# Squares, root and raw weights of a gated MLP prepared during the projection ahead of it, with its output tiles reloaded in four parts

## The chip, the cores and the metric

The kernel runs on one core of one Trainium2 chip. A core has a matrix engine (TensorE, PE in the profile), a vector engine (VectorE, DVE), an activation engine (ScalarE, ACT), a general engine (GpSimd, POOL) and an engine that issues most of the transfers (SyncE, SP). Each works through its own queue of instructions in order; semaphores tie the queues together. The metric is the device time of one execution in microseconds, as the median of several runs.

## The reference, cut to what matters

The model has two layers on x of 1024 rows (S) by 1024 columns (D): a mixer with its output projection, then a gated MLP with a causal convolution of width 3 (ConvGLU, called the FFN here), then a gated embedding add ("ple"). All is fp32.

```python
def rmsnorm(x, g):
    y = x * lax.rsqrt(jnp.mean(x * x, axis=-1, keepdims=True) + NORM_EPS)
    return y * g

def conv_glu(hn, w_in, conv_w, conv_b, w_out):           # FFN = 2816
    u, gate_in = jnp.split(hn @ w_in, 2, axis=-1)
    c = (conv_w[0] * shift_right(gate_in, 2) + conv_w[1] * shift_right(gate_in, 1)
         + conv_w[2] * gate_in + conv_b)
    return (jax.nn.gelu(c, approximate=False) * u) @ w_out

for each layer:
    h = h + mixer(rmsnorm(h, attn_norm))                 # ends in the output projection: o @ w_out
    h = h + conv_glu(rmsnorm(h, ffn_norm), ...)
    e = rmsnorm(p[layer] @ ple_w_proj, ple_norm)
    h = h + jax.nn.sigmoid(rmsnorm(h, ple_gate_norm) @ ple_w_gate) * e
```

## The kernel before

**Layout and split products.** Activations lie transposed: h is one tile of 128 partitions x 8 (the 1024 columns of D, KD = 8) x 1024 rows of the sequence, worked on in two halves of 512 (`lo` and `hi`, BW = 512). An fp32 operand is split into a rounded part and a rest (`split`, L169: a cast on ACT, L171, and a subtraction, L172, on POOL, or on the engine that the caller names). Each product of two operands is three matmuls (`mm3`, L190, recorded at L197): high by high, high by low, low by high.

**Output projection** (`out_proj`, L325). Eight tiles f of 128 output columns, two column blocks b of 512; each result is added into h by DVE at L332. The last three of its sixteen results are of the high half.

**Into the FFN.** `conv_glu` (L417) stores h to DRAM (L425), since the FFN works in the memory in which h lies, and calls `ffn_in` (L506). The product of h and w_in goes by a seven-product scheme on 2x2 blocks, so its operands are seven sums of quarters of the normalised h. `ffn_operands` (L438) makes them: for each half a root (`root`, L452: squares on ACT at L454 and L457, adds on DVE at L458, a matmul with ones at L460, a square root on ACT at L462, a reciprocal of 128x512 on DVE at L464), the normalised quarters (`normed`, L469, eight instructions a half), and then sums (L488, L490, L494, L499) and splits on DVE. The low half gives operands 0 and 1 (tiles `mh`, `ml`), the high half the rest (tiles `x`). The squares take tiles under the tag `x6`, in the pool of the seven operands, which is opened when the projection's operand tiles are freed. The weights get the same treatment in `seven_weights` (L356): raw loads (L363), the sums `s3` and three more on POOL (L375 to L380), and seven splits, two on POOL and five (`w6` and later) on DVE. The raw pool is opened in `ffn_in` too, after the projection.

**Out of the FFN.** `ffn_in` leaves its result u in DRAM (`md`, L548). Then h is loaded again into one tile (L432), after all its memory has come free, and `ffn_out` (L579) goes over u in groups of two tiles: loads `mraw` (L587), splits on POOL, and for each block b and, within it, each tile f a product and an add into h (L598). `ple` (L601) loads p into tiles of the weights' pool (`wraw`, L610) and splits them on POOL.

**Other parts that the change uses.** `sumsq_step` (L125) does one step of a sum of squares. `root` of the class (L146) makes the root otherwise: four narrow matmuls sum over partitions into a 128x4 tile (L149), square root (L151) and reciprocal (L152) work on that, and DVE multiplies it into a diagonal (L154). `spread` (L159) multiplies ones by that diagonal on PE, which puts the root into all 128 partitions of a PSUM tile (L161). `open_tail` (L306) opens the pools, among them `row` with six tiles and eight PSUM banks.

**Order.** The program writes down dependences; a scheduler sets each engine's order at build time, and memory that an earlier pool held can be used once the earlier users are done. `run` (L1665) calls all of this for both layers.

## Time and profile before

| | us |
|---|---|
| time, median of 3 runs | 3083.52 |
| lowest and highest run | 3079.57, 3084.25 |
| the profiled execution's own time | 3088.84 |
| its span | 3086.9 |
| PE busy | 2922.4 (95% of the span) |
| DVE, ACT, POOL busy | 2079.4, 1257.5, 1024.3 |
| mean granted clock of PE | 0.963 of full speed |

The profile is one execution, and its span begins and ends a little inside that execution's own time. The busy shares are over the whole span; the chain of waits and the timeline tell which engine a stretch waits for. The rows of the page and of the trace that matter stand two sections below, in numbered groups.

### The profile page before, as it was taken

What the parts mean: (1) busy time and instruction counts of PE and PEld (TensorE: products, weight loads), DVE (VectorE), ACT (ScalarE), POOL (GpSimd) and SP (SyncE); (2) the same over time, 40 slices, a digit from 0 to 9 for tenths busy, and PEclk for the clock granted to TensorE, in tenths of its full rate; (3) what the DMA queues carried; (4) which work ended last, traced back from release to release, by engine and by line L of the source; (5) the groups of instructions that cost most, each with busy time, mean ns of one, the idle gap of its engine ahead of it and who ended that gap; (6) DMA issues with size and microseconds to landing.
All of it is one profiled execution on the core that took longest, in us unless ns stands there. A gap on an engine that the chain in (4) does not pass through costs nothing. (4 is left out here: it accounts for less than half of the span.)

```text
span 3086.9 us, 40717 instructions
## 1 busy us (share of the span) xinstructions
PE 2922.4 (95%) x14510; PEld 2238.5 (73%) x14510; DVE 2079.4 (67%) x3202; ACT 1257.5 (41%) x2269; POOL 1024.3 (33%) x792
## 2 busy tenths in 40 slices
PE   8999999999599999999998899999789999999997
PEld 6777777678378888788886656556558888878876
DVE  6765657873787666544698677775397777655577
ACT  6433436672343333312544434343244333412274
POOL 4322421212244444544323500011134444544333
PEclk9998989999799999999999899999889999999998
DMA  4344565634122222532121300012212222243211
GB/s 139 115 140 119 156 200 141 157 83 160 48 86 82 82 82 72 181 92 79 62 89 55 110 15 23 19 38 96 72 55 82 82 82 82 97 155 99 62 60 55
DMA packets 221018, 286.07 MB, mean 93 GB/s; under 512 B 62256, under 2 KB 106800, under 8 KB 220816
## 3 DMA queue, kind: packets, MB, share of 16 engines
q1 hardware_dynamic: 215632, 272.99, 29.0%
q10 hardware_dynamic: 5184, 10.49, 0.9%
q8 instruction: 114, 1.87, 0.3%
q14 instruction: 88, 0.72, 0.1%
HBM read 200.50 MB, written 81.79 MB: 91 GB/s over the span
## 5 line engine op out<-in xcount | busy, mean ns | idle before, releaser
L197 PE MATMUL mm<-x,whi 128*128 128x512 f32 x1760 | 561.8, 398 | 17.9 <-DVE x L172 10.5
L172 POOL TENSOR_TENSOR wlo<-wraw,whi 128x512 fp32r<-128x512 f32 (+2 forms) x238 | 319.8, 1350 | 621.2 <-ACT whi L171 506.7
L197 PE MATMUL mm<-mh,whi 128*128 128x512 f32 x1056 | 419.1, 397 | 7.8 <-DVE h L598 7.6
L197 PE MATMUL mm<-mh,wlo 128*128 128x512 f32 x1056 | 418.8, 397 | 2.3 <-POOL wlo L172 2.3
L197 PE MATMUL mm<-ml,whi 128*128 128x512 f32 x1056 | 417.4, 395 | 0.0
L197 PE MATMUL mm<-xh,whi 128*128 128x512 f32 (+1 forms) x1016 | 406.7, 400 | 6.9 <-ACT xh L177 6.7
L197 PEld LDWEIGHTS mm<-x,whi 128*128 128x128 f32 x1760 | 333.1, 189 | 106.4 <-DVE x L172 20.3
L598 DVE TENSOR_TENSOR h<-h,mm 128x512 f32<-128x512 f32 x352 | 241.1, 688 | 237.7 <-PE mm L197 208.0
L197 PE MATMUL mm<-xh,wlo 128*128 128x512 f32 (+1 forms) x1016 | 399.5, 393 | 0.0
L197 PE MATMUL mm<-xl,whi 128*128 128x512 f32 (+1 forms) x1016 | 393.2, 394 | 0.5 <-DVE xl L178 0.5
L197 PE MATMUL mm<-x,wlo 128*128 128x512 f32 x880 | 347.1, 394 | 0.0
L171 ACT CAST whi<-raw 128x512 fp32r<-128x512 f32 x264 | 163.1, 619 | 356.8 <-PE mm L197 317.3
L171 ACT CAST whi<-wraw 128x512 fp32r<-128x512 f32 (+2 forms) x242 | 143.3, 596 | 343.1 <-PE mm L197 305.0
L197 PEld LDWEIGHTS mm<-mh,whi 128*128 128x128 f32 x1056 | 200.7, 190 | 55.9 <-DVE h L598 8.5
L197 PEld LDWEIGHTS mm<-ml,whi 128*128 128x128 f32 x1056 | 200.6, 190 | 47.7 <-issue 1.0
L197 PEld LDWEIGHTS mm<-mh,wlo 128*128 128x128 f32 x1056 | 200.3, 190 | 47.5 <-POOL wlo L172 3.2
L197 PEld LDWEIGHTS mm<-xh,whi 128*128 128x128 f32 x1016 | 195.4, 192 | 53.4 <-ACT xh L177 7.4
L197 PEld LDWEIGHTS mm<-xl,whi 128*128 128x128 f32 x1016 | 194.9, 192 | 46.0 <-issue 4.9
L197 PEld LDWEIGHTS mm<-xh,wlo 128*128 128x128 f32 x1016 | 195.0, 192 | 41.8 <-issue 2.1
L172 POOL TENSOR_TENSOR wlo<-raw,whi 128x512 fp32r<-128x512 f32 x88 | 130.7, 1486 | 270.9 <-ACT whi L171 270.7
L197 PEld LDWEIGHTS mm<-x,wlo 128*128 128x128 f32 x880 | 166.4, 189 | 36.3
L172 DVE TENSOR_TENSOR wlo<-raw,whi 128x512 fp32r<-128x512 f32 x176 | 153.3, 874 | 17.1 <-ACT whi L171 17.1
(414 smaller groups left out, 5234.8 us busy)
## 6 DMA issues: line engine op xcount, KB each, us to landing
raw<-in_ffn_w_in SPq DMA_DIRECT2D x176, 256.0 KB
wraw<-in_ffn_w_out SPq DMA_DIRECT2D x88, 256.0 KB
md<-u SPq DMA_DIRECT2D x88, 256.0 KB
mraw<-md SPq DMA_DIRECT2D x88, 256.0 KB
wraw<-in_hyb_w_in SPq DMA_DIRECT2D x52, 256.0 KB
hs<-h SPq DMA_DIRECT2D x32, 256.0 KB
h<-hs SPq DMA_DIRECT2D x32, 256.0 KB
wraw<-in_ple_w_gate SPq DMA_DIRECT2D x32, 256.0 KB
```

The lines of the kernel that those rows point to most:

```text
L171: nc.scalar.copy(out=hi, in_=src)
L172: (eng or nc.gpsimd).tensor_tensor(out=lo, in0=src, in1=hi, op=OP.subtract)
L197: nc.tensor.matmul(ps, lhsT=w, rhs=x, start=first and i == 0, stop=last and i == len(seq) - 1)
L598: nc.vector.tensor_tensor(out=h[:, f, bs], in0=h[:, f, bs], in1=ps, op=OP.add)
```

## The change

There are five edits. (1) `ffn_operands` makes its sums of squares by `sumsq_step`, with one square tile in the `row` pool, and its roots by `root` and `spread`, so that the normalising instructions read the root from PSUM. (2) The pool of raw weights is opened ahead of the projection's operand and closed after `ffn_in`. (3) The late splits of the weights (five of seven, `late`) go to POOL for the first pair of tiles, and stay on DVE for the others. (4) The h that is reloaded lies in four tiles of two column groups each (`Rows` finds the right one); `ffn_out` goes over f outside and b inside, and the splits of its group 0 (c == 0) go to DVE. (5) `ple` loads p into tiles under the tags `sq` and `sd`. `run` opens the raw pool for layer 1 as the last lines of the diff show it for layer 0.

```diff
+class Rows:
...
+    def __getitem__(self, at):
+        p, k, cols = at
+        if isinstance(k, slice):
+            n = k.start // 2
+            return self.tiles[n][p, slice(k.start - 2 * n, k.stop - 2 * n), cols]
+        return self.tiles[k // 2][p, k % 2, cols]
...
-    def sumsq_step(self, pool, acc, src, first):
+    def sumsq_step(self, pool, acc, src, first, bufs=2):
...
-            sq = pool.tile([P, BW], F32, name="sq", bufs=2)[:, :src.shape[1]]
+            sq = pool.tile([P, BW], F32, name="sq", bufs=bufs)[:, :src.shape[1]]
...
-    def seven_weights(self, wp, rp, srcs):
+    def seven_weights(self, wp, rp, late, srcs):
...
-        def split(x, eng=nc.vector):
+        def split(x, eng=late):
...
+    def open_raw(self, ctx):
+        self.rp = ctx.enter_context(self.tc.tile_pool(reuse_waits="tile", name="raw", bufs=RAWS))
+
-    def conv_glu(self, h, layer, c_h):
+    def conv_glu(self, h, layer, c_h, c_raw):
...
-        h = self.pool_tile(c_h, f"h2_{layer}", "right")
+        c_raw.close()
+        pool = c_h.enter_context(tc.tile_pool(reuse_waits="tile", name=f"h2_{layer}", bufs=1, side="right"))
+        h = Rows([pool.tile([P, 2, S], F32, name=f"h2_{k}") for k in range(0, KD, 2)])
...
             acc = row.tile([P, BW], F32, name="row")
             for k in range(KD):
-                if k == 0:
-                    nc.scalar.activation(out=acc, in_=h[:, k, bs], func=AF.Square)
-                else:
-                    sq = xp.tile([P, BW], F32, name="sq", tag="x6", bufs=KD)
-                    nc.scalar.activation(out=sq, in_=h[:, k, bs], func=AF.Square)
-                    tt(out=acc, in0=acc, in1=sq, op=OP.add)
-            ps = self.pm.tile([P, BW], F32, name="mm")
-            nc.tensor.matmul(ps, lhsT=self.ones, rhs=acc, start=True, stop=True)
-            sd = row.tile([P, BW], F32, name="row")
-            nc.scalar.activation(out=sd, in_=ps, func=AF.Sqrt, scale=1.0 / D, bias=self.eps[:, 0:1])
-            r = row.tile([P, BW], F32, name="row")
-            nc.vector.reciprocal(out=r, in_=sd)
-            return r
+                self.sumsq_step(row, acc, h[:, k, bs], k == 0, 1)
+            return self.spread(self.pm, self.root(row, self.pm, acc, D, tag="row", bufs=6))
...
-        rp = ctx.enter_context(tc.tile_pool(reuse_waits="tile", name="raw", bufs=RAWS))
...
-        def weights(tiles):
-            return self.seven_weights(self.wp, rp, [[w_in[layer, f][:, H * k:H * k + H] for k in range(2)] for f in tiles])
+        def weights(tiles, late=nc.vector):
+            return self.seven_weights(self.wp, self.rp, late, [[w_in[layer, f][:, H * k:H * k + H] for k in range(2)] for f in tiles])
...
-            gates = self.seven(ep, xs, weights([NFT + f for f in tiles]), outs(gate))
+            late = nc.vector if i else nc.gpsimd
+            gates = self.seven(ep, xs, weights([NFT + f for f in tiles], late), outs(gate))
             if i == 0:
 
-                ups = self.seven(ep, xs, weights(tiles), outs(up))
+                ups = self.seven(ep, xs, weights(tiles, late), outs(up))
...
-                    self.split(mh[b], ml[b], raw)
+                    self.split(mh[b], ml[b], raw, eng=None if c else nc.vector)
...
-            for b in range(NBLK):
-                bs = slice(b * BW, (b + 1) * BW)
-                for f in range(KD):
+            for f in range(KD):
+                for b in range(NBLK):
+                    bs = slice(b * BW, (b + 1) * BW)
...
-                praw = wp.tile([P, BW], F32, name="praw", tag="wraw", bufs=self.wbufs[0])
+                praw = sp.tile([P, BW], F32, name="praw", tag=("sq", "sd")[k])
...
-                with ExitStack() as c_op:
-                    self.open_operand(c_op, scratch=False)
-                    self.out_proj("hyb_w_out", o, load(t["x"]), h)
-                h = self.conv_glu(h, 0, c_h)
+                with ExitStack() as c_raw:
+                    self.open_raw(c_raw)
+                    with ExitStack() as c_op:
+                        self.open_operand(c_op, scratch=False)
+                        self.out_proj("hyb_w_out", o, load(t["x"]), h)
+                    h = self.conv_glu(h, 0, c_h, c_raw)
```

What this does to the engines' queues shows in three places. The names: `mh` and `ml` are block tiles (the high and low part of operands 0 and 1, or a gate product), `xh` and `xl` the projection's operand, `whi` and `wlo` split weights, `row` a sum of squares, `sq` a square, `raw` and `s` raw weights and their sums. A row with xN stands for N alike in a row. Lines of the kernel after the change are higher: L211 is L197, L186 is L172, L346 is L332, L147 is L458, L477 is L469.

On PE, from the last product of layer 0's output projection into the FFN's first product, before:

```order
L197 MATMUL mm<-xl,whi 128x512
L197 MATMUL mm<-xh,wlo 128x512
L460 MATMUL mm<-row,ones 128x512 x2
L197 MATMUL mm<-mh,whi 128x512
L197 MATMUL mm<-ml,whi 128x512
L197 MATMUL mm<-mh,wlo 128x512
```

and after:

```order
L211 MATMUL mm<-xl,whi 128x512
L211 MATMUL mm<-xh,wlo 128x512
L163 MATMUL mm<-ones,row 128x1 x4
L175 MATMUL mm<-diag,ones 128x512
L211 MATMUL mm<-mh,whi 128x512
L211 MATMUL mm<-ml,whi 128x512
L211 MATMUL mm<-mh,wlo 128x512
...
L211 MATMUL mm<-mh,wlo 128x512
L163 MATMUL mm<-ones,row 128x1 x4
L175 MATMUL mm<-diag,ones 128x512
L211 MATMUL mm<-x_7760,whi 128x512
```

Both roots (one matmul with ones each) stood together ahead of the FFN's first product; now the first root stands there, and the second stands 24 matmuls (operands 0 and 1) later, ahead of the first matmul of an operand `x`.

On DVE, from the last adds of that projection to the first operand of the high half, before:

```order
L332 TENSOR_TENSOR h<-h,mm 128x512 x16
L458 TENSOR_TENSOR row<-row,sq 128x512 x7
L464 RECIPROCAL row<-row 128x512
L458 TENSOR_TENSOR row<-row,sq 128x512
L469 SCALAR_TENSOR_TENSOR h<-h,cols,row 128x512 x3
...
L469 SCALAR_TENSOR_TENSOR h<-h,cols,row 128x512 x2
L458 TENSOR_TENSOR row<-row,sq 128x512
L172 TENSOR_TENSOR ml<-h,mh 128x512 x2
L458 TENSOR_TENSOR row<-row,sq 128x512
L172 TENSOR_TENSOR wlo<-raw,whi 128x512
L458 TENSOR_TENSOR row<-row,sq 128x512
...
L464 RECIPROCAL row<-row 128x512
```

and after:

```order
L346 TENSOR_TENSOR h<-h,mm 128x512 x3
L166 RECIPROCAL sdt<-sdt 128x4
L168 TENSOR_TENSOR diag<-ident,sdt 128x512
L147 TENSOR_TENSOR row<-row,sq 128x512
L477 SCALAR_TENSOR_TENSOR h<-h,cols,mm 128x512 x3
L186 TENSOR_TENSOR ml<-h,mh 128x512 x3
...
L186 TENSOR_TENSOR ml<-h,mh 128x512 x2
L147 TENSOR_TENSOR row<-row,sq 128x512 x5
L166 RECIPROCAL sdt<-sdt 128x4
L168 TENSOR_TENSOR diag<-ident,sdt 128x512
L477 SCALAR_TENSOR_TENSOR h<-h,cols,mm 128x512 x2
```

The adds of the squares of the low half have moved up among the adds into h; of the high half's adds five stand together behind the splits of the low half, and the weight splits that stood between them are gone from this place.

On POOL, at the start of layer 0's projection (L1477 and L1582, after it L1486 and L1591, are the end of the mixer: copies, and products with the gate), before:

```order
L1477 COPY stacks<-stacks 64x256 x10
L172 TENSOR_TENSOR wlo<-wraw,whi 128x512 x2
L1582 TENSOR_TENSOR ml<-ml,gate 128x512
L172 TENSOR_TENSOR wlo<-wraw,whi 128x512
L1582 TENSOR_TENSOR ml<-ml,gate 128x512
L172 TENSOR_TENSOR wlo<-wraw,whi 128x512
L1582 TENSOR_TENSOR ml<-ml,gate 128x512
L172 TENSOR_TENSOR wlo<-wraw,whi 128x512 x2
L1582 TENSOR_TENSOR ml<-ml,gate 128x512
L172 TENSOR_TENSOR wlo<-wraw,whi 128x512 x10
L375 TENSOR_TENSOR s_7954<-raw 128x512
```

and after:

```order
L1486 COPY stacks<-stacks 64x256 x10
L389 TENSOR_TENSOR s_7966<-raw 128x512
L390 TENSOR_TENSOR raw<-raw 128x512
L186 TENSOR_TENSOR wlo<-wraw,whi 128x512 x2
L1591 TENSOR_TENSOR ml<-ml,gate 128x512
L186 TENSOR_TENSOR wlo<-wraw,whi 128x512
L1591 TENSOR_TENSOR ml<-ml,gate 128x512
L186 TENSOR_TENSOR wlo<-wraw,whi 128x512
L1591 TENSOR_TENSOR ml<-ml,gate 128x512 x2
L186 TENSOR_TENSOR wlo<-wraw,whi 128x512 x12
L186 TENSOR_TENSOR wlo<-raw,whi 128x512
```

Two sums of raw weights have moved from behind the projection's weight splits to the front, and the fifth split of a projection weight has moved from ahead of the last gate product to behind it.

## Rows read from the trace of the kernel before

**Rows 1.** The page, part 1: busy us, share of the span, instructions

```profile
PE 2922.4 (95%) x14510; PEld 2238.5 (73%) x14510; DVE 2079.4 (67%) x3202; ACT 1257.5 (41%) x2269; POOL 1024.3 (33%) x792
```

**Rows 2.** Waits of PE by releaser: line waited for: us in total, times, longest

```profile
PE mm L460 <- DVE row L458: 56.8, 4, 20.8
...
PE mm L197 <- DVE h L598: 7.6, 2, 4.0
...
PE mm L197 <- POOL wlo L172: 2.3, 2, 1.3
```

**Rows 3.** Timeline, PE, layer 0: start, us, instruction, count [idle before <-releaser]

```profile
790.04 2.07 PE L460 MATMUL mm<-row,ones 128*128 128x512 f32 x2 [7.04 <-DVE row L458]
...
812.95 2.08 PE L460 MATMUL mm<-row,ones 128*128 128x512 f32 x2 [20.84 <-DVE row L458]
...
854.33 0.50 PE L197 MATMUL mm<-x,whi 128*128 128x512 f32 x1 [0.24 <-DVE x L172]
```

**Rows 4.** Timeline, DVE, the same stretch

```profile
783.65 6.34 DVE L458 TENSOR_TENSOR row<-row,sq 128x512 f32<-128x512 f32 x7
...
796.69 2.06 DVE L469 SCALAR_TENSOR_TENSOR h<-h,cols,row 128x512 f32<-128x512 f32 x3
...
807.40 0.69 DVE L458 TENSOR_TENSOR row<-row,sq 128x512 f32<-128x512 f32 x1
...
820.43 1.41 DVE L469 SCALAR_TENSOR_TENSOR h<-h,cols,row 128x512 f32<-128x512 f32 x2
...
824.22 1.76 DVE L469 SCALAR_TENSOR_TENSOR h<-h,cols,row 128x512 f32<-128x512 f32 x1
...
840.37 4.27 DVE L172 TENSOR_TENSOR x<-h,x 128x512 fp32r<-128x512 f32 x4 [1.64 <-ACT x L171]
```

**Rows 5.** Timeline, ACT, the same stretch

```profile
784.37 0.63 ACT L457 ACTIVATE sq<-h 128x512 f32<-128x512 f32 x1 [15.77 <-DVE row L458]
```

**Rows 6.** Timeline, POOL, the same stretch

```profile
810.02 4.00 POOL L375 TENSOR_TENSOR s<-raw 128x512 f32<-128x512 f32 x1 [13.90 <-DVE wlo L172]
...
822.62 2.81 POOL L172 TENSOR_TENSOR wlo<-raw,whi 128x512 fp32r<-128x512 f32 x1 [7.26 <-ACT whi L171]
```

**Rows 7.** Timeline, PE, narrow matmuls of a root elsewhere in the kernel

```profile
1710.89 1.05 PE L149 MATMUL mm<-ones,row 128*128 128x1 f32 x8 [0.56 <-DVE row L133]
```

**Rows 8.** Lines L151, L154, L161: xcount: ns min/median/max, first and last start, forms

```profile
L151 ACT ACTIVATE sdt<-mm,eps x5: 262/263/264, 1712.0 to 3077.4; 128x4 f32<-128x4 f32 x3, 128x2 f32<-128x2 f32 x2
...
L154 DVE TENSOR_TENSOR diag<-ident,sdt x5: 424/692/1057, 1712.5 to 3077.9; 128x512 f32<-128x512 f32 x3, 128x256 f32<-128x256 f32 x2
...
L161 PE MATMUL mm<-diag,ones x10: 544/592/766, 1721.2 to 3079.1; 128*128 128x512 f32 x6, 128*128 128x256 f32 x4
```

**Rows 9.** Timelines, SP, POOL, DVE, PE, start of layer 0's projection

```profile
676.14 15.16 SPq L183 DMA_DIRECT2D wraw<-in_hyb_w_out  x4
...
700.64 2.99 POOL L172 TENSOR_TENSOR wlo<-wraw,whi 128x512 fp32r<-128x512 f32 x2
703.60 1.74 POOL L1582 TENSOR_TENSOR ml<-ml,gate 128x512 f32<-128x512 f32 x1
...
699.45 1.95 DVE L1579 SCALAR_TENSOR_TENSOR ml<-tr,cols,bv 64x256 f32<-64x256 f32 x4
...
703.06 0.39 PE L197 MATMUL mm<-xh,whi 128*128 128x512 f32 x1
703.28 0.39 PE L197 MATMUL mm<-xh,wlo 128*128 128x512 f32 x1
```

**Rows 10.** Timeline of SP, then the chain that ended last, layer 1

```profile
2700.04 0.94 SPq L587 DMA_DIRECT2D mraw<-md  x2
2702.75 9.52 SPq L432 DMA_DIRECT2D h<-hs  x16
...
2694.15 1.74 POOL wlo L172
...
2697.82 4.85 DMA md<-u
```

14 lines of the change are left out of this document (9 added, 5 removed).

## The prediction

> **What bounds the kernel now.** I read the busy shares first: TensorE (PE) is busy 95% of a span of 3086.9 us, so whatever the change gains has to come out of PE's idle time [rows 1]. Next the waits of PE by releaser. The largest by far is the root matmul of the FFN waiting for the sum of squares, 56.8 us in four waits; the change touches two more, 7.6 us at the start of ffn_out (for h) and 2.3 us at the start of ple (for a split on POOL) [rows 2]. Then the timeline, to see what these waits are made of. In layer 0 PE ends the output projection at 783.0 (790.04 less 7.04), waits 7.04 us for the first root and, after it, 20.84 us for the second [rows 3]. On DVE that stretch is seven adds (from 783.65, 6.34 us), root, splits of the low half until 807.40, five more adds, a reciprocal of 128x512, and at 820.43 the first operand of the high half [rows 4]. ACT shows the cause of the late adds: its squares could not start before 784.37, after 15.77 us of idle, though the low half of h is complete some 16 us before the projection ends (three results of the high half, 24 matmuls of 0.22 us each, come behind it [rows 9]): each has a tile in memory that the projection's last matmul still reads [rows 5]. From 820.43 DVE makes the high half's operands back to back, and PE runs dry behind it in small steps until 854.33 [rows 3, 4]. So the bound between 783.0 and 854.33 is DVE's chain, not PE, and time is won only by what brings 854.33 forward. Layer 1 repeats it: the other two of the four waits are 56.8 - 7.04 - 20.84 = 28.9 us.
>
> **Squares and root of the low half.** After the change the seven adds stand among the adds of the projection, ahead of its last three, so at 783.0 the sum is there. The root is now four narrow matmuls, 1.05 us [rows 7], a square root of 128x4, 0.26, a reciprocal of that size, for which I take 0.2 (between nothing and the square root's 0.26), the diagonal, 0.69, and the spreading matmul, two passes of 0.59 that overlap, about 1.0 [rows 8]: 3.2 us, 3.4 with the handoffs. The low half starts at 783.0 + 3.4 = 786.4 instead of 796.69, 10.3 us sooner. In layer 1 the square root needs an activation table to be loaded, and it does in the kernel before too; there I take the same gain.
>
> **The low half's splits** take 807.40 - 796.69 = 10.7 us [rows 4]; I add 1.0 us for one POOL instruction that falls into them (see below): end at 798.1.
>
> **Squares of the high half.** One tile makes square and add alternate: 0.63 + 0.69 and about 0.1 of handoff, 1.4 us a step [rows 4, 5], where before the squares lay ready and DVE put a late split between two adds. Five adds are left after the low half. The first is ready; the second's square stands on ACT behind a weight cast that waits for PE to finish the second product. I estimate that it ends 3.5 us after the first begins, and three steps follow: 798.1 + 3.5 + 4.2 = 805.8. The root's 3.4 us give 809.2 for the first high operand, against 820.43: 11.2 us sooner. The 24 matmuls of products 0 and 1, which stood behind the second root, now run between the roots, in time in which PE idles anyway.
>
> **The high half** takes 854.33 - 820.43 = 33.9 us now [rows 3, 4]. Two late splits of 0.6 us leave DVE for POOL: -1.2. A POOL instruction beside dense DVE work is not free: while POOL's ran for 2.81 us in place of 1.3 to 1.5 [rows 6, 9], the DVE instruction at 824.22 took 1.76 us, where three of its kind in 2.06 are 0.69 each [rows 4]. That is 1.0 us a piece, and I count two more of them than now: +2.0. PE has five more matmuls behind the last operand, since its order is another, at 0.22 us each [rows 9]: +1.1. Net 11.2 + 1.2 - 2.0 - 1.1 = 9.3 us a layer, **18.6 us in two**. Bounds: with no collision and without the stall of 1.64 us in today's phase [rows 4], 17 us a layer; with 4.0 us for every POOL instruction, as at 810.02 [rows 6], and a high half that waits for them, 3 us.
>
> The trace thus shows DVE and POOL delaying each other by about 1 us an instruction [rows 4, 6]. The Trainium skill ("SBUF — State Buffer", the reading of its diagram) says why this speaks against moving splits to POOL: the SBUF port pair that the two share is an exclusive lock, and the later of a GpSimd instruction and a DVE instruction with two SBUF inputs waits for the whole of the other. By that rule alone a split moved from DVE's 0.6 us costs DVE up to a POOL instruction's 1.3 to 1.5, and the sum would be some 2 us smaller for each layer; the rows agree with the rule in kind.
>
> **Early raw weights.** They remove loads from behind the last store of h; POOL's two sums of them move from behind the projection into its idle time. That costs something at layer 0's projection start, where the order on POOL changes: the split of the fifth weight tile now stands behind the last gate product (1.74 us at 703.60), not ahead of it [rows 9]. PE wants that split at 703.28; today it ends at about 702.1 (half of 2.99 after 700.64). With the product from 701.4, when DVE has made its input (699.45 plus 1.95), to 703.1, it ends at 704.6 [rows 9]: **+1.4 us**, bounds 0 and 4. The three raw loads now ahead of the first projection weights I count at nothing: those weights go out at 676.14, 27 us before that split is wanted [rows 9], and a load is worth about 1 us.
>
> **h in four tiles, and the order of ffn_out.** Today the reload goes out at 2702.75, when the store of the last output, issued at 2697.82, has landed after 4.85 us [rows 10]; PE waits 3.6 us for it (7.6 less layer 0's 4.0 [rows 2]). The first of the four tiles waits for that store no longer, only for the issues ahead of it on SP, which end at 2700.98 [rows 10]; the following ones still wait for it, as the order of the changed kernel has it. So 1.75 us a layer by the reload alone. The splits of group 0, moved from POOL to DVE, act both ways: POOL's split at 2694.15 stands on the chain that leads to this store [rows 10] and comes sooner, but on DVE four splits of 0.7 us now stand ahead of the last outputs. I take 2 a layer, **4 us**, bounds -4 and 7.6. The loop order f outer, b inner matches the order of the loads and moves no PE work. Block 0 of h is complete later, but nobody needs it at once: ple multiplies p first, 96 matmuls, 21 us.
>
> **p in tiles of its own** takes the split off the start of ple: 2.3 us in two waits [rows 2], of which I take **1.5**, bounds 0 and 2.3.
>
> **Sum:** 18.6 + 4 + 1.5 - 1.4 = 22.7 us. The profiled execution took 3088.84, so 3066.1 by it; it lies 5.3 us above the median of 3083.52, and nothing in the terms depends on that, so the forecast is **3060.8 us**.
>
> **Rivals.**
> *Less collision.* DVE's chain runs free of POOL and of the cast stalls: 17 us a layer and all of the 7.6 us: 34 + 7.6 + 2 - 1 = 43, 3041 us. For it: the spread result lies in PSUM, so the 16 normalising instructions read one SBUF operand less. Against: POOL has as many instructions in the phase as before or more.
> *The single square tile holds the second root.* If a step costs 2.5 us rather than 1.4, because casts come between, five adds take 5 us longer: 22.7 - 2 x 5 = 12.7, 3071 us. For it: ACT's queue is in order and its casts wait for PE.
> *No measurable change.* The high half stays the bound and becomes longer by what the roots save, as when the POOL collisions double: within 6 us of 3083.5. That covers also the case that the squares are held by another wait and the adds don't come early; against it, the order shows only h and the one tile in front of them.
> *Slower: POOL becomes the bound.* Seven products need 84 matmuls, 84 x 0.225 = 18.9 us, and eleven POOL instructions when all late splits are there. At over 18.9 / 11 = 1.72 us each PE waits for POOL. Two sets a layer go that way, 22 instructions, 44 in all: at 2.3 us the excess is 0.58 x 44 = 26 us, more than the gain. At 2.81, as seen [rows 6], it is 48 us: 22.7 - 48, 3109 us. Against it: at 1.5 us a piece [rows 9] POOL has room, and after the high half DVE is less dense.
>
> **Numbers.** Chances: forecast (a gain of 14 to 30 us) 0.50; less collision 0.17; square tile 0.15; no change 0.11; slower 0.07. The three gains make faster 0.82. A difference of 0.2%, 6 us, is about what a measurement here can tell from none. The range covers the forecast, the square-tile rival and most of the less-collision rival and stops where the no-change case begins: 3041 to 3078.
>
> **What would show it.** Right: PE's two waits for the root are about 2 us (for the diagonal) and some 8 to 11 us; the low half starts 3.4 us after the projection, the high half some 26 us after it, the last operand wait ends about 61 us after it instead of 71; no reciprocal of 128x512 at that place. Wrong: adds in the high half 2.5 us apart (square tile); waits of PE on POOL's wlo of more than a few us (slower rival); operand instructions on DVE of 1.7 us more often than four times a layer (collision).

## The result and the profile after

The changed kernel takes 3050.62 us (median of 6 runs, 3036.43 to 3060.0) against 3079.65 us for the kernel before (median of 6, 3074.47 to 3084.25): a ratio of 0.9898, 95% interval 0.9868 to 0.9928, 29 us less. The forecast was 22.7 us less, inside a range that holds the result. Of the executions below, one of the kernel with a second square tile and the late splits on DVE took 7709.59 us, more than twice its other three, and is left out of its median.

The page's busy line after the change, part 1 (it answers [rows 1]):

```profile
PE 2925.0 (96%) x14542; PEld 2238.0 (73%) x14542; DVE 2072.6 (68%) x3194; ACT 1256.2 (41%) x2269; POOL 1035.7 (34%) x804
```

PE has almost the same work as before, in a span of 3053.9 instead of 3086.9 us. The waits of PE after the change (engine, line waited for: us in total, times, longest us), to be read against [rows 2]:

```profile
PE mm L163 <- DVE row L147: 13.6, 2, 6.8
...
PE mm L211 <- DVE x L186: 12.2, 14, 1.9
...
PE mm L175 <- DVE diag L168: 7.5, 5, 2.2
...
PE mm L211 <- DVE h L607: 3.4, 2, 1.9
...
PE mm L211 <- POOL wlo L186: 1.2, 2, 1.0
```

The 56.8 us of waits for a root's sum have become 13.6 us, with 6.4 us more for the diagonals of the same four roots, and 7.6 us for h have become 3.4. Where the time went is seen better by stretches of PE, cut at the first and last matmul of each stage in the two timelines:

| stretch of PE, us | before | after | difference | forecast |
|---|---|---|---|---|
| mixer of layer 0, to the projection's first matmul | 690.32 | 680.93 | -9.39 | 0 |
| projection, layer 0 | 92.69 | 94.65 | +1.96 | +1.4 |
| projection's end to the end of FFN's input products, layer 0 | 473.72 | 470.19 | -3.53 | -9.3 |
| ffn_out, layer 0 | 253.35 | 249.94 | -3.41 | -2.75 |
| ple, mixer of layer 1 | 612.49 | 610.42 | -2.07 | 0 |
| projection, layer 1 | 90.23 | 89.86 | -0.37 | 0 |
| projection's end to the end of FFN's input products, layer 1 | 479.86 | 472.47 | -7.39 | -9.3 |
| ffn_out, layer 1 | 247.66 | 241.01 | -6.65 | -2.75 |
| ple and the end | 139.37 | 137.47 | -1.90 | 0 |

The five stretches for which the forecast has a term give 19.0 us, the rest 13.7. Up to 669 us after the change, where the first raw load is issued, the five queues hold the same instructions in the same order in both kernels, and the mixer's 9.4 us are there by then, so they are not the edits'. Most of them arise between 200 and 300 us, where PE's granted clock was 0.86 before and 0.97 after (start and end, length; PE busy us and count, PEld, DVE, ACT, POOL, clock, DMA share, GB/s; first before, then after):

```profile
200.00:300.00 100.00, 96.52 (x609) 73.44 (x608) 67.92 (x127) 35.28 (x58) 24.73 (x21) 0.86 0.32 96
```

```profile
200.00:300.00 100.00, 95.81 (x655) 72.20 (x654) 73.93 (x138) 40.81 (x67) 24.73 (x21) 0.97 0.37 110
```

In the thirteen traces of this study other than that of before the mixer takes 678.8 to 694.0 us, and in two of them this piece is slow as well. The traced run of before is also 9.2 us above its median, that of after 5.0.

Inside the third row of the table, layer 0 after the change, first PE (timeline: start us, us, instruction, count, idle before it and what ended it):

```profile
777.96 2.08 PE L175 MATMUL mm<-diag,ones 128*128 128x512 f32 x2 [1.60 <-DVE diag L168]
...
799.44 1.87 PE L163 MATMUL mm<-ones,row 128*128 128x1 f32 x8 [6.83 <-DVE row L147]
...
807.42 0.80 PE L211 MATMUL mm<-x,whi 128*128 128x512 f32 x1 [2.75 <-ACT x L185]
...
831.96 0.50 PE L211 MATMUL mm<-x,whi 128*128 128x512 f32 x1 [1.74 <-DVE x L186]
...
835.32 0.50 PE L211 MATMUL mm<-x,whi 128*128 128x512 f32 x1 [1.94 <-DVE x L186]
...
840.51 0.50 PE L211 MATMUL mm<-x,whi 128*128 128x512 f32 x1
```

then DVE and POOL in the same stretch:

```profile
780.07 2.06 DVE L477 SCALAR_TENSOR_TENSOR h<-h,cols,mm 128x512 f32<-128x512 f32 x3 [1.57 <-PE mm L175]
...
791.64 0.68 DVE L147 TENSOR_TENSOR row<-row,sq 128x512 f32<-128x512 f32 x1
...
798.69 0.69 DVE L147 TENSOR_TENSOR row<-row,sq 128x512 f32<-128x512 f32 x1 [0.70 <-ACT sq L146]
...
804.71 1.41 DVE L477 SCALAR_TENSOR_TENSOR h<-h,cols,mm 128x512 f32<-128x512 f32 x2 [2.17 <-PE mm L175]
...
824.43 0.68 DVE L508 TENSOR_TENSOR h<-h,t 128x512 f32<-128x512 f32 x1
825.18 3.32 DVE L186 TENSOR_TENSOR x<-h,x 128x512 fp32r<-128x512 f32 x2
828.43 1.78 DVE L508 TENSOR_TENSOR h<-h,t 128x512 f32<-128x512 f32 x1
...
833.52 4.16 DVE L186 TENSOR_TENSOR x<-h,x 128x512 fp32r<-128x512 f32 x5
839.08 1.38 DVE L186 TENSOR_TENSOR x<-h,x 128x512 fp32r<-128x512 f32 x1 [1.40 <-ACT x L185]
```

```profile
820.11 6.16 POOL L186 TENSOR_TENSOR wlo<-raw,whi 128x512 fp32r<-128x512 f32 x1 [24.05 <-ACT whi L185]
826.35 1.60 POOL L394 TENSOR_TENSOR raw<-raw 128x512 f32<-128x512 f32 x1
827.92 1.74 POOL L186 TENSOR_TENSOR wlo<-raw,whi 128x512 fp32r<-128x512 f32 x1
...
838.60 1.31 POOL L186 TENSOR_TENSOR wlo<-raw,whi 128x512 fp32r<-128x512 f32 x1 [3.88 <-ACT whi L185]
```

and ACT ahead of DVE's instruction at 825.18:

```profile
824.01 0.62 ACT L185 CAST whi<-raw 128x512 fp32r<-128x512 f32 x1 [1.41 <-PE mm L211]
824.53 1.67 ACT L185 CAST x<-h 128x512 fp32r<-128x512 f32 x3
```

The projection ends at 775.58. The low half starts 4.5 us after it (780.07), the first operand of the high half comes from DVE 29.1 us after it (804.71) and reaches PE at 31.8 (807.42). Up to 824 DVE's instructions follow each other every 0.60 us, and POOL's split, issued at 820.11, does not get on. At 825.11 DVE pauses for 0.07 us: the cast of `x` that its next split needs runs on ACT from 824.53, behind the cast of a weight, and is ready just too late. From there the two engines alternate, each DVE instruction with two inputs in SBUF takes 1.7 us, and PE waits three times, the last time until 835.32. That is not yet the last operand: five splits are still to come, the last of them (839.08) after a wait of 1.40 us for its cast, and PE takes it up at 840.51, 64.9 us after the projection's end (71.3 before).

### The profile page after: what moved, and what is told of

Same layout as the page of the kernel before. It is cut to its first block, busy times and chain, and to the rows that moved or that the text cites. A ratio compares the mean times of both kernels' runs of the same rounds, so it can differ in the third digit from the quotient of the medians.

```text
span 3053.9 us, 40783 instructions
## 1 busy us (share of the span) xinstructions
PE 2925.0 (96%) x14542; PEld 2238.0 (73%) x14542; DVE 2072.6 (68%) x3194; ACT 1256.2 (41%) x2269; POOL 1035.7 (34%) x804
## 5 line engine op out<-in xcount | busy, mean ns | idle before, releaser
L211 PE MATMUL mm<-x,whi 128*128 128x512 f32 x1760 | 566.9, 402 | 21.4 <-DVE x L186 12.2
L186 POOL TENSOR_TENSOR wlo<-wraw,whi 128x512 fp32r<-128x512 f32 (+2 forms) x238 | 318.6, 1346 | 558.0 <-ACT whi L185 500.8
L211 PE MATMUL mm<-mh,whi 128*128 128x512 f32 x1056 | 416.2, 395 | 6.4 <-DVE h L607 3.4
L211 PE MATMUL mm<-ml,whi 128*128 128x512 f32 x1056 | 417.7, 396 | 3.9 <-DVE ml L186 3.9
L211 PEld LDWEIGHTS mm<-x,whi 128*128 128x128 f32 x1760 | 335.2, 191 | 115.4 <-DVE x L186 20.2
L211 PE MATMUL mm<-mh,wlo 128*128 128x512 f32 x1056 | 417.1, 395 | 0.0
L211 PE MATMUL mm<-xh,whi 128*128 128x512 f32 (+1 forms) x1016 | 405.2, 399 | 7.2 <-ACT xh L191 7.2
L211 PE MATMUL mm<-xh,wlo 128*128 128x512 f32 (+1 forms) x1016 | 398.9, 393 | 1.2 <-POOL wlo L186 1.2
L211 PE MATMUL mm<-xl,whi 128*128 128x512 f32 (+1 forms) x1016 | 393.1, 394 | 0.5 <-DVE xl L192 0.5
L211 PE MATMUL mm<-x,wlo 128*128 128x512 f32 x880 | 349.4, 397 | 0.0
L186 POOL TENSOR_TENSOR wlo<-raw,whi 128x512 fp32r<-128x512 f32 x104 | 158.2, 1521 | 368.8 <-ACT whi L185 368.5
L211 PEld LDWEIGHTS mm<-mh,whi 128*128 128x128 f32 x1056 | 200.0, 189 | 55.8 <-ACT mh L185 5.9
L211 PEld LDWEIGHTS mm<-ml,whi 128*128 128x128 f32 x1056 | 199.9, 189 | 51.3 <-DVE ml L186 5.6
L211 PEld LDWEIGHTS mm<-xh,whi 128*128 128x128 f32 x1016 | 194.5, 191 | 53.6 <-ACT xh L191 8.0
L211 PEld LDWEIGHTS mm<-mh,wlo 128*128 128x128 f32 x1056 | 199.8, 189 | 44.1
L211 PEld LDWEIGHTS mm<-xl,whi 128*128 128x128 f32 x1016 | 194.0, 191 | 46.0 <-issue 4.6
L211 PEld LDWEIGHTS mm<-xh,wlo 128*128 128x128 f32 x1016 | 194.1, 191 | 43.7 <-POOL wlo L186 2.1
L211 PEld LDWEIGHTS mm<-x,wlo 128*128 128x128 f32 x880 | 167.9, 191 | 38.1
L934 ACT ACTIVATE w<-s 128x512 f32<-128x512 f32 (+1 forms) x192 | 94.0, 491 | 166.8 <-PE s L932 147.5
```

Source lines behind the costliest of these rows:

```text
L186: (eng or nc.gpsimd).tensor_tensor(out=lo, in0=src, in1=hi, op=OP.subtract)
L211: nc.tensor.matmul(ps, lhsT=w, rhs=x, start=first and i == 0, stop=last and i == len(seq) - 1)
L934: nc.scalar.activation(out=w[:, :n], in_=s[:, :n], func=AF.Exp, scale=MLA_SCALE)
```

## The experiments

Each is the changed kernel with one edit, unless the text says otherwise. "High start" is the first product of the high half after the projection's end (31.8 and 31.5 us in layers 0 and 1 of the changed kernel; 41.4 and 42.1 before), "FFN-in" the end of FFN's input products after it (470.2 and 472.5; 473.7 and 479.9 before). Runs with one time were made for their trace; their times are not compared.

**Late splits back on DVE.**

```diff
-            late = nc.vector if i else nc.gpsimd
+            late = nc.vector
```

> The changed kernel with the late weight splits of the first pair of tiles back on DVE. In the changed kernel (layer 0) PE's last wait for an operand of the high half ends 59.7 us after the projection, and FFN's input products end 470.2 us after it; five DVE instructions from 825.18 took 8.34 us, where 0.6 us each is their pitch elsewhere, while POOL's stood at 1.6 to 6.2 us. Theory of collision: with five POOL splits fewer beside DVE's dense stretch, DVE's chain is 3 to 5 us shorter, the last wait ends at 55 to 57 us, and the products end at 465 to 467. Rival (it is POOL's sums of raw weights that collide, and they stay): last wait within 1 us of 59.7, and DVE pays 0.6 us for each split that lands in the high half. Second rival (PE's backlog and clock decide, not the last wait): the last wait moves and the end of the products does not, 470 within 1 us.

High start 31.1 and 31.6; FFN-in 461.6 and 466.7, that is 8.6 and 5.8 us sooner. In layer 0 the three late waits are gone: behind 39.8 us after the projection PE waits only twice, 0.2 us each. But not because POOL has left: its first split of that stretch is still there, and waits through DVE's whole dense stretch.

```profile
818.45 14.63 POOL L186 TENSOR_TENSOR wlo<-raw,whi 128x512 fp32r<-128x512 f32 x1 [24.01 <-ACT whi L185]
```

It gets on when DVE comes to two small memsets and an instruction with one input in PSUM. In layer 1 DVE pauses sooner (0.45 us, for a cast), and the same split is through after 6.19 us; behind it POOL has one sum and then waits for a split of DVE, so that the alternation ends soon.

**A second square tile for the high half.**

```diff
             acc = row.tile([P, BW], F32, name="row")
+            if bs is hi:
+                pair = [row.tile([P, BW], F32, name="sq", bufs=1), row.tile([P, BW], F32, name="row")]
             for k in range(KD):
-                self.sumsq_step(row, acc, h[:, k, bs], k == 0, 1)
+                if bs is lo or k == 0:
+                    self.sumsq_step(row, acc, h[:, k, bs], k == 0, 1)
+                else:
+                    sq = pair[k % 2]
+                    nc.scalar.activation(out=sq, in_=h[:, k, bs], func=AF.Square)
+                    tt(out=acc, in0=acc, in1=sq, op=OP.add)
```

> The changed kernel with a second tile for the squares of the high half, used in turn with the first. In the changed kernel the five adds behind the low half take 7.7 us (791.64 to 799.38) with DVE waiting for ACT before four of them, 3.4 us in all. Theory of the single tile: with two tiles the adds take 4.3 to 5 us, the first high operand comes about 3 us sooner, and the last wait ends at 56 to 57 us after the projection instead of 59.7; the input products end 2 to 3 us sooner than 470.2. Rival (the squares wait for weight casts ahead of them on ACT, which wait for PE): the adds still take 7 us or more, and nothing moves by over 1 us.

High start 29.9 and 30.3, so 2.0 and 1.2 us sooner: the five adds take 5.8 us (793.29 to 799.06) instead of 7.7, less than the theory gave: a weight cast stands between the squares on ACT, and two of the adds take 1.34 and 1.57 us instead of 0.69, beside a split and a sum on POOL. FFN-in is 460.6 and 463.7, 9.6 and 8.7 us sooner, far more than the adds explain. The rest is POOL again. The late splits are on POOL here as in the changed kernel, yet DVE's stretch has no pause, and POOL's split starves to its end:

```profile
819.80 12.18 POOL L186 TENSOR_TENSOR wlo<-raw,whi 128x512 fp32r<-128x512 f32 x1 [22.09 <-ACT whi L185]
```

```profile
824.11 0.69 DVE L515 TENSOR_TENSOR h<-h,t 128x512 f32<-128x512 f32 x1
824.71 1.29 DVE L186 TENSOR_TENSOR x<-h,x 128x512 fp32r<-128x512 f32 x2
```

So a pause of 0.07 us on DVE goes with some 8 us: from the first high product to the end of FFN-in it takes 438.4 and 441.0 us in the changed kernel, 430.7 and 433.4 here. The other traces without padding whose products stand in the same order agree, with one exception: where the split on POOL took 6.14 to 6.16 us, it was 438.2 to 438.5 us in layer 0 and 440.9 to 441.4 in layer 1; where it took 12.17 to 14.64, it was 430.5 to 430.7 and 433.3 to 433.4. The exception is layer 1 of the run before this one, with 6.19 us and 435.1. In the second trace of the changed kernel the pause is only 0.03 us. A pause is not always needed: in the kernel before, POOL got in ahead of the normalising instruction at 824.22 [rows 4, 6] without one, so what lets it in is not settled in full.

**Roots as before, squares early.**

```diff
-            return self.spread(self.pm, self.root(row, self.pm, acc, D, tag="row", bufs=6))
+            ps = self.pm.tile([P, BW], F32, name="mm")
+            nc.tensor.matmul(ps, lhsT=self.ones, rhs=acc, start=True, stop=True)
+            sd = row.tile([P, BW], F32, name="row")
+            nc.scalar.activation(out=sd, in_=ps, func=AF.Sqrt, scale=1.0 / D, bias=self.eps[:, 0:1])
+            r = row.tile([P, BW], F32, name="row")
+            nc.vector.reciprocal(out=r, in_=sd)
+            return r
```

> The changed kernel with its roots made as before (one matmul with ones, square root and reciprocal of 128x512, root in SBUF), and nothing else undone. From the last add into a sum to the first normalised quarter the changed kernel takes 4.5 us (low) and 5.3 us (high) in layer 0, where the kernel before took 6.7 and 7.5. Theory: both roots lie on the chain, each costs 2.2 us more, the last wait ends 4.4 us later (64 us after the projection) and the input products end 3 to 4.5 us later, at 473 to 475. Rival (the low root is covered, since DVE waits for ACT later anyway): 2.2 us later, 62. Second rival (the root's form matters more through the port, since the normalising instructions read SBUF again): over 6 us later.

```profile
810.32 2.08 PE L474 MATMUL mm<-row,ones 128*128 128x512 f32 x2 [21.58 <-DVE row L147]
...
858.47 0.50 PE L211 MATMUL mm<-x,whi 128*128 128x512 f32 x1 [0.90 <-DVE x L186]
```

High start 34.8 and 35.6, 2.9 and 4.2 us later; FFN-in 473.0 and 479.8, 2.8 and 7.4 later. FFN-in of layer 0 fits the first theory; the last wait does not, since it ends 70.6 and 71.9 us after the projection, not 64, over 6 us later as the second rival has it. The built order differs, too: both roots stand together on PE again, with the low products behind the second, and without the root's small tile the pitch of PE is that of the kernel before (last section), so the comparison is of the root, of this order and of the pitch together.

**Squares in the tiles of before, roots by diagonals kept.**

```diff
-                self.sumsq_step(row, acc, h[:, k, bs], k == 0, 1)
+                if k == 0:
+                    nc.scalar.activation(out=acc, in_=h[:, k, bs], func=AF.Square)
+                else:
+                    sq = xp.tile([P, BW], F32, name="sq", tag="x6", bufs=KD)
+                    nc.scalar.activation(out=sq, in_=h[:, k, bs], func=AF.Square)
+                    tt(out=acc, in0=acc, in1=sq, op=OP.add)
```

> The changed kernel with its squares in the tiles of before (tag x6), which the projection's last matmuls still read, and the roots by diagonals kept. Theory (the squares' tiles are the larger part of the gain): the seven low adds come behind the projection again, the low half starts 6.3 us later, at 10.8 us after the projection instead of 4.5; the high half then has its squares ready and its adds take 4 to 5 us instead of 7.7, so the last wait ends 3 to 4 us later, at 63, and the input products end at 473. Rival (the whole chain is pushed by the low adds): 6.3 us later at the last wait, 66, and 476 at the end. Second rival (the single tile costs as much as it brings): no difference over 1 us at the last wait.

PE's wait for the low root is back, and the low half starts 8 us later:

```profile
787.57 1.87 PE L163 MATMUL mm<-ones,row 128*128 128x1 f32 x8 [7.22 <-DVE row L477]
```

Yet the high start is only 1.9 and 2.0 us later (33.7 and 33.4), because the high half's adds find their squares ready. FFN-in comes sooner than in the changed kernel (464.5 and 466.9), since POOL's split starves here too (12.19 us). So the early squares, with one tile, bring 2 us a layer to the high half: most of what they win at the low root the single tile takes back.

**The raw weights' pool opened after the projection.**

```diff
-                    self.open_raw(c_raw)
                     with ExitStack() as c_op:
                         self.open_operand(c_op, scratch=False)
                         self.out_proj("hyb_w_out", o, load(t["x"]), h)
+                    self.open_raw(c_raw)
                     h = self.conv_glu(h, 0, c_h, c_raw)
```

> The changed kernel with the pool of raw weights opened after the projection again, so that loads, sums and splits of the first pair's weights come behind it. Theory 1 (the early sums cost the start of layer 0's projection): the projection takes 92.7 us from its first matmul instead of 94.6 and has no wait for a split on POOL. Theory 2 (the weights' splits on POOL meet DVE's dense stretch): with all of them behind the projection, at least eight POOL instructions fall into the transition, the first product waits for POOL's split, and FFN's input products end 3 to 10 us later than 470 us after the projection. Rival (weights are never late): the end stays within 1 us of 470 or, where no POOL instruction enters DVE's dense stretch, of 461.

(The same in layer 1.) The projection of layer 0 takes 93.45 us, 1.2 less, with no wait for POOL: theory 1, though 0.8 us more than before stay. The high start is at 38.9 and 38.3, 7.1 and 6.8 us later. FFN-in is 469.7 in layer 0, where POOL starves later on (12.22 us), and 479.2 in layer 1, where it gets in. Theory 2 so holds in layer 1 alone, and PE's first product waits for a cast on ACT, not for POOL. The 7 us arise in the low half, and the rows of DVE and POOL show how:

```profile
775.53 2.06 DVE L477 SCALAR_TENSOR_TENSOR h<-h,cols,mm 128x512 f32<-128x512 f32 x3 [0.62 <-PE mm L175]
777.51 5.07 DVE L186 TENSOR_TENSOR ml<-h,mh 128x512 fp32r<-128x512 f32 x3
```

```profile
777.39 1.27 POOL L389 TENSOR_TENSOR s<-raw 128x512 f32<-128x512 f32 x1
778.74 1.61 POOL L390 TENSOR_TENSOR raw<-raw 128x512 f32<-128x512 f32 x1
```

In the changed kernel, and in the kernel before, the same three splits are

```profile
782.05 1.89 DVE L186 TENSOR_TENSOR ml<-h,mh 128x512 fp32r<-128x512 f32 x3
```

```profile
798.67 1.89 DVE L172 TENSOR_TENSOR ml<-h,mh 128x512 fp32r<-128x512 f32 x3
```

With the raw weights late, POOL works through sums and splits all the while. Three splits, with two inputs in SBUF, take 5.07 us instead of 1.89; three normalising instructions, whose root lies in PSUM, take 2.06 as always. The low half takes 19.6 us on DVE instead of 11.6. In the kernel before, the raw weights came late as well, but POOL was done with the first of them at 796.1, just ahead of the low half, and idle until 810.0: only with the squares early does the low half come into POOL's way. So the early raw weights mostly keep what the early squares would lose again. Undoing them costs 7 us a layer at the high start, undoing the squares 2 and the roots with their order 3 to 4; these prices do not add up, since the whole change brought 9.6 and 10.7 there.

**One tile for the reloaded h.**

```diff
-        pool = c_h.enter_context(tc.tile_pool(reuse_waits="tile", name=f"h2_{layer}", bufs=1, side="right"))
-        h = Rows([pool.tile([P, 2, S], F32, name=f"h2_{k}") for k in range(0, KD, 2)])
+        h = self.pool_tile(c_h, f"h2_{layer}", "right")
```

> The changed kernel with the reloaded h in one tile again. Where ffn_out starts, PE waits for h 1.0 to 2.7 us in the ten such places of the five traces with four tiles, 4.0 and 3.6 us in the two of the kernel before. Theory (the four tiles let the first load go before the last store has landed): the wait is 3.4 to 4.2 us in both layers. Rival (the splits of group 0 on DVE bring that store forward, and that is the gain): the wait stays at 1.0 to 2.7 us.

**Group 0's splits back on POOL.**

```diff
-                    self.split(mh[b], ml[b], raw, eng=None if c else nc.vector)
+                    self.split(mh[b], ml[b], raw)
```

> The changed kernel with the splits of ffn_out's group 0 on POOL again. Theory (the tiles alone shorten the wait for h): PE's wait at the start of ffn_out stays at 1.0 to 2.7 us. Rival (DVE's splits matter): 3 us or more, or a new wait of PE for a split on POOL of 1 to 3 us ahead of it.

PE's waits for h, first with one tile, then with the splits on POOL:

```profile
PE mm L211 <- DVE h L606: 3.2, 2, 2.3
```

```profile
PE mm L211 <- DVE h L607: 7.8, 2, 4.0
```

With one tile the two waits are 0.93 and 2.30 us, as with four; with the splits on POOL they are 3.81 and 4.03, as in the kernel before. The four tiles bring nothing that can be seen; the splits on DVE bring all of it. The two layers' ffn_out agree: from FFN-in's end to its last product they take 501.3 us in sum before, 491.3 and 491.9 in the two traces of the changed kernel, 491.2 with one tile and 499.4 with the splits on POOL. Both theories that credited the tiles fell.

**PE kept busy ahead of the high root.** Thirty matmuls of operand tiles, whose result is not used, behind operand 1.

```diff
+        for n, _ in enumerate(gates):
+            if n == 1:
+                ps = self.pm.tile([P, BW], F32, name="mm")
+                for i in range(30):
+                    nc.tensor.matmul(ps, lhsT=xs[0][0][0][:, :P], rhs=xs[1][1][H - 1], start=True, stop=True)
```

> The changed kernel with 30 matmuls more, whose result is not used, behind operand 1 and ahead of the high half's root, where PE otherwise waits 6.8 us. In the changed kernel PE's clock is at 1.2 GHz at that root (1.01 us between the spreading matmul's two passes) and until 822.1, 46.5 us after the projection. Theory (the idle ahead of the root takes the clock down): with PE busy there the passes are 0.5 us apart, the four narrow matmuls and the spread take 1.9 us less, the first product of the high half comes 1.5 to 2 us sooner than 31.8 us after the projection, and the products end 2 to 6 us sooner than 470. Rival (the clock stays down, or falls at the next wait): the passes stay 1.0 us apart, or the gain ahead of the first high product is under 0.5 us. Second rival (the added matmuls get in the way): the high root comes later by up to 7 us.

```profile
798.86 1.05 PE L163 MATMUL mm<-ones,row 128*128 128x1 f32 x8 [0.99 <-DVE row L147]
799.77 1.18 PE L579 MATMUL mm<-ml,mh 128*128 128x512 f32 x4
801.21 2.08 PE L175 MATMUL mm<-diag,ones 128*128 128x512 f32 x2 [0.26 <-DVE diag L168]
```

The narrow matmuls took 1.05 instead of 1.87 us, at the full clock of 2.4 GHz, but the granted clock fell to half at 801.0, and the spread after the next short wait took 2.08 as without them. High start 32.3 and 32.7, no gain; the scheduler also put other products between the high half's. FFN-in 470.6 and 474.0. The theory fell; whether a steadier filler would help was not tried.

**The changed kernel again, and both mends together.** The second square tile and the late splits on DVE in one kernel, timed side by side.

> The changed kernel itself once more. In its first trace POOL's split of a weight enters DVE's dense stretch in both layers: three waits of PE of 0.9 to 2.0 us late in the high half, and 438 and 441 us from the first high product to the end of FFN's input products. Traces of kernels that are alike in that place show 438 to 441 with these waits and 430 to 433 without, and two of them one layer with and one without. Theory (whether POOL gets in is chance from run to run): runs differ by about 8 and 16 us, and this trace may show 430 to 433 in a layer. Rival (the order of the changed kernel fixes it): 438 and 441 again, in both layers.

> The changed kernel with a second square tile for the high half and the late splits on DVE. Theory: the gains of both add up where they are separate: from the projection's end to the end of FFN's input products 458 to 461 us in layer 0 and 462 to 466 in layer 1, instead of 470.2 and 472.5, and the run is 12 to 20 us shorter than the changed kernel's. Rival (the second tile's 1.9 us and the absent collision are the same gain, once): 460 to 462, as with either alone.

The changed kernel takes 3059.14 us (5 runs, 3051.09 to 3064.16), and its trace has 438.5 and 441.1 us with POOL's split at 6.16 us again: its order brings the pause each time it was traced, as the rival has it, and chance from run to run is not shown; a kernel that differs from it elsewhere (group 0 on POOL) had it in one layer and not in the other. With both mends it is 3037.93 (3 runs, 3036.19 to 3040.62, no overlap), 21 us less; FFN-in 459.0 and 462.2, inside the theory's ranges and 1.6 and 1.5 us sooner than with the second tile alone. So nearly all of it is one gain, the absent alternation, which either mend brings in layer 0.

**Padding.** Mean pitch of 128x512 matmuls at the full clock differs by stage, in stretches without any wait: before the change 644 in 150 us in layer 0's ffn_out (from 1300 us), 663 in layer 1's (from 2715). In the built program the address of a matmul's moving operand less that of its weights, modulo 256 bytes, is 96 in the first and 0 in the second. The edit pads constants and the root's small tile, and puts an unused tile of 96 bytes on the right side of memory, so that the difference is a multiple of 128 everywhere:

```diff
-        self.cols = cp.tile([P, NCOLS], F32, name="cols")
+        self.cols = cp.tile([P, 320], F32, name="cols")[:, :NCOLS]
+        pad = self.ctx.enter_context(tc.tile_pool(reuse_waits="tile", name="pad", bufs=1, side="right")).tile([P, 24], F32, name="pad")
+        nc.vector.memset(pad, 0.0)
...
-        sd = pool.tile([P, g], F32, name="sdt", bufs=2)
+        sd = pool.tile([P, 16], F32, name="sdt", bufs=2)[:, :g]
```

> The changed kernel with padding alone: every tile that a matmul reads starts at the same address modulo 128 bytes; no instruction differs but for one memset. In the traces the mean pitch of a 128x512 matmul at the full clock is 226.7 ns in the ffn_out of layer 1, where the built program has its two operands at equal addresses modulo 128, 229 to 230 where they are 64 apart (the projection and FFN of layer 0 in the changed kernel), and 233.3 where they are 32 apart (ffn_out of layer 0, the projection of layer 1). Theory (the offset sets the pitch): 226.5 to 227.5 everywhere; ffn_out of layer 0 takes 7 us less (243 instead of 250), the projection of layer 1 2.6 less, FFN's inputs 6 and 9 less, the run 22 to 36 less. Rival (the pitch follows the weights' side of memory or the layer): no stage changes by over 1 us.

> The changed kernel with a second square tile, late splits on DVE, and the padding. Theory: the gains add up to 35 to 55 us below the changed kernel, 2995 to 3015 us. Rival (PE's clock gives part of it back, since PE is then busy with the same work in less time): under 30 us below it.

Busy time in stretches of PE without a wait (columns as above), inside ffn_out of layer 0 and FFN's inputs of layer 1, first the changed kernel, then the padded one:

```profile
1300.00:1450.00 150.00, 150.00 (x645) 120.67 (x644) 73.71 (x108) 29.57 (x52) 63.90 (x52) 1.00 0.29 90
...
2300.00:2500.00 200.00, 200.00 (x865) 162.11 (x865) 142.90 (x198) 79.41 (x129) 86.26 (x61) 1.00 0.25 81
```

```profile
1300.00:1450.00 150.00, 150.00 (x647) 121.62 (x646) 74.01 (x108) 28.66 (x50) 65.71 (x52) 1.00 0.28 91
...
2300.00:2500.00 200.00, 200.00 (x884) 165.58 (x884) 141.29 (x203) 80.68 (x131) 93.04 (x64) 1.00 0.26 83
```

In layer 1, where the padding makes the difference 0, the pitch falls to 226.7 ns: FFN's inputs take 8.7 us less from the first high product, the projection 2.5 less, as expected. In layer 0 the padded difference is 128, and the pitch is 232.4 everywhere: by the pitch 1 us less in ffn_out, and in the traces 3.7 and 1.2 more in FFN's inputs and the projection, against the theory, which took 128 for enough. The whole is 3048.02 us (5 runs, 3043.88 to 3059.79) against 3059.14, so 11 us less where 22 to 36 were expected. With both mends and the padding it is **3026.89** (5 runs, 3023.05 to 3027.71), a ratio to the kernel before of 0.9811 (0.9798 to 0.9825): 59 us less than before and 32 less than the changed kernel, short of the 35 to 55 expected and the best measured here. A padding that makes the difference 0 in layer 0 as well was not run.

## Why the prediction was right, point by point

**What bounds the kernel.** Right: between the projection and the first products of the FFN it is DVE's chain, and PE's idle time there, to the last wait for an operand, fell from 36.9 to 23.9 us in layer 0.

**Low root.** Predicted 3.4 us from the projection's end; 4.5 measured. The sum was there, as said: the narrow matmuls follow the projection's last one without a wait. PE's granted clock fell to half (1.2 GHz) at 777.8, during the wait for the diagonal, so the spread took 2.08 us for its two passes, taken as 1.0, and that is the whole miss.

**Low splits and adds.** End of the low splits predicted 15.1 us after the projection, 16.1 measured; the five adds predicted 7.7 us in all, 7.7 measured (791.64 to 799.38). The single tile works as described. That POOL stays out of these splits, but for one instruction, the forecast took from the kernel before; here it hangs on the early raw weights (below).

**High root.** Predicted 3.4, measured 5.3: narrow matmuls 1.87 and spread 2.07 us, at the low clock. The high half so starts 29.1 us after the projection instead of 26.2, 8.3 us sooner than before instead of 11.2.

**High half.** Predicted 33.9 - 1.2 + 2.0 = 34.7 us, and the last wait for an operand 61 us after the projection. PE's last long wait ends at 59.7, but that is luck: it is not for the last operand, as it was in the kernel before. The last operand reaches PE 35.8 us after DVE began the first one, 64.9 us after the projection, 6.4 us sooner than before instead of the 10.4 forecast (7.4 sooner in layer 1). Of this miss, the largest of the prediction, 3.0 us are the two roots (the spreads and the high root's narrow matmuls, at the low clock) and 1.1 the high half. There the collision was mis-sized: 5.3 us (five DVE instructions from 825.18 took 8.34 us instead of 3.0), then 1.4 of waiting for a cast and 0.7 beside POOL at 839.08, 7.4 where 2.0 were forecast. Most of the excess is made good, as the stall of 1.64 us and two collisions of 1.0 us each (one of them in [rows 4]), which the forecast kept, are gone.

**PE behind the last operand.** Five more matmuls were forecast, 1.1 us, and counted from the first matmul of the last operand there are five more, 1759 against 1754. To FFN-in's end they take 405.26 us instead of 402.41 in layer 0 and 407.93 instead of 407.95 in layer 1. What is left beside the five is the pitch, which no term had: a mean of 229.4 ns before and 230.4 after in layer 0 (+1.7 us), 232.6 and 231.9 in layer 1 (-1.2). So of 6.4 us won at the last operand 3.5 reach FFN-in's end in layer 0, and of 7.4 all in layer 1, against 9.3 each.

**Early raw weights.** The cost at the projection's start was right in kind and place: POOL's split keeps PE waiting 0.97 us, and the stage is 1.96 longer. The other 0.9 is the pitch (226.8 to 228.9 ns), which no term had. Two experiments part them: without the wait (raw weights late) the projection takes 93.45 us, with the wait and the pitch of before (roots as before) 93.86. What the early pool brings was missed: the rule on POOL and DVE was applied to what moves to POOL in the high half and not to what leaves POOL's way in the low half, and without it 7 us a layer at the high start would be lost again.

```profile
694.96 0.50 PE L211 MATMUL mm<-xh,wlo 128*128 128x512 f32 x1 [0.97 <-POOL wlo L186]
```

**The rule of the port.** The prediction set the Trainium skill's rule ("SBUF — State Buffer", the reading of its diagram) beside 1 us a collision. The Trainium skill says on the same page ("Who interferes with whom") that a DVE instruction with at most one SBUF input, outside the two-port modes, does not contend with GpSimd, and the late raw weights agree, 2.06 us beside 5.07. Where the Trainium skill and the runs part: it has the lock held for one whole instruction, which alone would let POOL in after one of DVE's; here POOL's split took 12.18 and 14.63 us, against 1.3 by itself, through some twenty of them back to back. By the measurement, the splits on POOL cost 8.6 and 5.8 us in the two layers where POOL got in, and nothing that shows where it did not (two square tiles).

**ffn_out.** 4 us forecast; the two waits for h fell by 2.15 and 2.12, 4.3 in sum. The size of the waits was right by luck and the cause wrong: not the four tiles (1.75 of the 2), but the splits on DVE, whose effect the prediction had left open in sign. The two stages became 10.1 us shorter, against 5.5 with ple's part. In layer 1 some 3 us of that came from the clock: behind the wait of 3.6 us twelve matmuls ran at a pitch of 0.43 us before, behind 1.5 us none. That part is not firm: in the second trace of the changed kernel seven did, behind 2.2 us, and the stage was 2.3 us longer.

**ple.** Both waits for POOL's split are gone, 0.97 and 1.33 us, 2.3 against 1.5. They stood at the last weights of ffn_out, 21 us ahead of ple's first product, not at its start as the prediction has it. No run undoes the p tiles alone, so that it is they, and not the order of ffn_out, that took these waits away is not shown.

**The sum.** In the traces the edits give 19.0 us against 22.7: 7.7 too little in FFN-in, 4.6 too much in ffn_out, and 0.6 at the projection. So the number is near for a mixture of reasons, and the prediction was right in its chain and wrong in several sizes. The medians differ by 29.0 and, in the second timing, 27.1 us, 8 to 10 more than the edited stretches show. This is no merit of the forecast: in the two traces the rest is mostly the clock in the mixer, where nothing was edited; whether the untraced runs of before mostly have that slow piece stays open, as only one of them was traced.

## What to carry to other kernels

Before work is moved between VectorE and GpSimd, mark which VectorE instructions have two inputs in SBUF and look at what GpSimd does beside them: here a dense row of them either starves GpSimd or, after a pause of 0.07 us, is slowed nearly threefold. A preparation is best tested by undoing one part at a time: the part that was meant to pay (squares) costs 2 us when it is undone, the part that was to cost nothing (raw weights) 7, and the prices do not add up. A mark in a trace must be the same thing in both kernels: the last wait was for the last operand before the change and for an earlier one after it. A wait's price is read with what PE runs after it: the matmuls still to come and the clock at which they start.

## What the runs showed of the hardware

A split on GpSimd that takes 1.3 us by itself waits out a whole row of VectorE instructions with two inputs in SBUF: it took 6.16 us where VectorE paused, 12.2 to 14.6 where it did not. And the pitch of a 128x512 matmul at the full clock goes with where its two operands lie. By the difference of their addresses modulo 256 bytes, in the stages that have one difference throughout, it is 226.7 to 226.9 ns (0), 228.9 (64), 232.4 (128), 233.3 (96 and 224) and 234.3 (160). Only the padding experiment moved addresses and nothing else, to 0 and 128; which property of the addresses decides, and why, stays open. A kernel's pools can so lose 1% of a stage by a tile of 16 bytes: with the root's small tile layer 0's projection has 228.9 ns, without it (before, and with the roots as before) 226.8.
